# Low halves of split weight tiles: an engine subtraction, or a copy and an accumulating DMA

## The chip, the cores and the metric

The kernel runs on one core of one Trainium2 chip. A core has a matrix engine (TensorE, PE in the profile), two elementwise engines (VectorE or DVE, ScalarE or ACT), a programmable engine (GpSimd or POOL) and SyncE (SP), which here only issues DMAs. Each takes its instructions in the order of the program; an instruction that has to wait holds up everything behind it on its engine. DMAs can be issued from SP, ACT or GpSimd; all of them are carried out by the core's 16 DMA engines.

The metric is the device time of one execution in microseconds (us), the median of repeated runs.

## The reference

A trunk of two decoder layers over 512 tokens of width 1024, in float32. What the chip spends its time on is cut to this:

```
layer 0:  u = rmsnorm(x);  proj = u @ w_in            # 1024 -> 7200 columns
          y = SSD scan (16 heads);  o = forgetting attention (16 heads)
          x = x + rmsnorm(concat(y, o) @ w_out)       # 2048 -> 1024
layer 1:  u = rmsnorm(x);  val, gate, z = split(u @ w_in)   # 1024 -> 3 * 2048
          h = val * sigmoid(gate)
          h = causal depthwise conv, 31 taps, over 2048 channels
          h = silu(layernorm(h)) * silu(z)
          x = x + rmsnorm(h @ w_out)                  # 2048 -> 1024
```

## The kernel before, in words

**Split products.** TensorE multiplies here in the rounded type float32r. To keep float32 accuracy each operand is split in two: `hi`, its rounding, and `lo = value - hi`. A product is three matmuls: hi by hi, hi by lo, lo by hi (`mm3`). Activations are split as they are made, weights as they are loaded, so every weight tile (128 partitions x 1024 elements, 512 KB) goes this way: SP issues its load into a raw buffer `wr` (`wload`, L124); ACT rounds it into the first half of a tile `w` (L107, a CAST); DVE or GpSimd subtracts, `w[lo] = wr - w[hi]` (L108); PE reads both halves. The table of jobs says which engine subtracts: DVE and GpSimd by turns in layer 0, mostly DVE in layer 1 (`ENG1 = V`, `GLO`). Twelve half-size tiles `ws` at the border of the layers are treated alike.

**Buffers.** Raw tiles come from a pool of two buffers. `w` tiles share a pool of seven with other tiles of 8 KB per partition (the gate inputs `zs` and `sz`, attention weights `ph` and `pl`, at the start the input `x` and scratch `junk`). A raw buffer is free when both the rounding and the subtraction have read it. `split_to` calls for the splits of the next two jobs, or more, ahead of the job that runs, at a raised priority (`HP`).

**Jobs and order.** The products are a list of jobs, one weight tile each, mostly 24 matmuls. PE's order is written by hand; the other engines' orders are made by a scheduler from priorities, at build time. Beside the jobs run "chains", stepped a fixed number of steps per chunk of products: the scan and the attention in layer 0, and in layer 1 the convolution. The convolution's taps are dealt out: DVE adds taps in PSUM (L723, L727), ACT multiplies and GpSimd adds others in SBUF (L666 and L681), a few go to PE. When all 16 channel tiles are done, their sums (L749, L753) give the layer norm's statistics (L813 to L826), and only then can the last product, by `w_out`, begin.

**Stages**, by the profile's time: start 0 to 60 us; layer 0's projections with scan and attention 60 to 555; its output product 555 to 616; border of the layers to 674; layer 1's projections with the convolution 674 to 1003 (called *the convolution stage* below); the statistics to 1016; the last product to 1101; the end.

At the start x's rows are normalized, transposed by PE (`uT`) and split by ACT and DVE into eight pairs `uh`, `ul` (L236, L237), numbered uh_123 to uh_130 in the listings below. PE's first product (`dtf`) needs all eight in turn.

Of the kernel before, what the change touches and what calls it, by code (L numbers as in the profile page):

```python
# [12 lines left out]
ALU = mybir.AluOpType  # L13
# [3 lines left out]
S = 512  # L17
# [19 lines left out]
def trunk(  # L37
# [7 lines left out]
    V, G, A, T = nc.vector, nc.gpsimd, nc.scalar, nc.tensor  # L45
# [3 lines left out]
    cp = ctx.enter_context(tc.tile_pool(name="const", bufs=1))  # L49
    rp = ctx.enter_context(tc.tile_pool(name="raw", bufs=2))  # L50
    qp = ctx.enter_context(tc.tile_pool(name="q", bufs=7))
# [54 lines left out]
    def split(hi, lo, src, hi_eng, lo_eng):  # L106
        hi_eng(hi, src)  # L107
        lo_eng.tensor_tensor(lo, src, f32(hi), ALU.subtract)  # L108
# [11 lines left out]

    # ---------------------------------------------------------------- weight tiles, loaded and split ahead of their use
    def wload(w, r0, nk, c0, n):
# [3 lines left out]
        return raw  # L126

    def wsplit(raw, nk, n, eng, small=False):
        if small:
            hl = [[t2("ws", F32R) for _ in range(2)] for _ in range(2)]  # L130
            for i in range(2):
                split(hl[0][i], hl[1][i], raw[:, i * S : (i + 1) * S], A.copy, eng)
            return [lambda k, t=t: t[k // 4][:, k % 4 * P : (k % 4 + 1) * P] for t in hl]
        hl = q8("w", [2, 1024])
        split(hl[:, 0, : nk * n], hl[:, 1, : nk * n], raw[:, : nk * n], A.copy, eng)
        v = hl[:, :, : nk * n].rearrange("p a (k f) -> p a k f", k=nk)
        return [lambda k, a=a: v[:, a, k, :] for a in range(2)]

    jobs = []
# [28 lines left out]
    def chunks():  # L168
        """Runs the next job, one chunk of products a step."""
        i = state["run"]  # L170
        split_to(i + 1)
        first = True
        for _ in jobs[i].run(*jobs[i].w):
            if first:
                split_to(i + 1 + ahead.get(i, 2))
                first = False
            yield
        state["run"] = i + 1
# [3 lines left out]
    def run(n, chain=None, pace=0.0):  # L182
        """Runs n jobs; after each chunk `pace` steps of the chain on average."""
        for _ in range(n):
            for _ in chunks():
                debt[0] += pace
                while debt[0] >= 1.0:
                    debt[0] -= 1.0
                    if chain is not None and next(chain, None) == "wait":
                        debt[0] = 1.0 - pace  # L190
                        break
# [4 lines left out]

    # ---------------------------------------------------------------- norms
    def rstd_of(ss, n):
# [13 lines left out]
    def scaled(dst, xs):  # L212
        """dst = xs / rms(xs), xs being the parts of the rows."""
        s2 = col("s2", 2)
        for i, t in enumerate(xs):
            sumsq(t, s2[:, i : i + 1])
        if len(xs) == 2:
            V.tensor_tensor(s2[:, 0:1], s2[:, 0:1], s2[:, 1:2], ALU.add)
        r = rstd_of(s2[:, 0:1], D)
        for t, u in zip(xs, dst):  # L220
            V.tensor_scalar(u, t, r, None, ALU.mult)
# [16 lines left out]

    # ---------------------------------------------------------------- inputs and constants
    xq = [q8("x", [2, D], F32) for _ in range(2)]  # L240
# [28 lines left out]

    # dt and forget-gate columns of the input projection  # L270
    raw = rp.tile([P, 1024], F32, tag="wr", name=nm("wr"))
# [45 lines left out]
    def conv_columns():  # L317
        v3 = t2("v3")
        nc.sync.dma_start(v3[:124, :].rearrange("p (a c) -> p a c", a=4),
                          o_conv_w[0].rearrange("k (t c) -> (k t) c", c=P).rearrange("(a p) c -> p a c", p=124))  # L320
        yield
        pb = bank("cw")
        for a in range(4):
            T.transpose(pb[:, a * 124 : (a + 1) * 124], v3[:124, a * P : (a + 1) * P], ident[:124, :124])
        V.tensor_copy(cw, pb[:, :496])
        # a shift common to all channels leaves the layer norm as it is: take the bias' mean out
        bm = col("bm")
        V.tensor_reduce(bm, c1[:, o_cb1 : o_cb1 + 16], AX.X, ALU.add)
        pb = bank("bm")
        mm(pb[:, 0:1], ones, bm, True, True)  # L330
        bs = col("bs")
        V.tensor_scalar(bs, pb[:, 0:1], -1.0 / 2048, None, ALU.mult)
        V.tensor_scalar(c1[:, o_cb1 : o_cb1 + 16], c1[:, o_cb1 : o_cb1 + 16], bs, None, ALU.add)
        yield

    # ---------------------------------------------------------------- jobs of layer 0
    uh = [t2("uh", F32R) for _ in range(KT)]
# [107 lines left out]

    # ---- layer norm / residual end of a layer
    RES = 6
# [4 lines left out]
    def out_proj(w, stages, nk, gpost, resid, done, hooks):  # L452
        """stages: (fn, lead) pairs; the last fn(k) gives (hi, lo) of the k-th 128 rows of the contraction."""
        hl = {}
# [79 lines left out]

    # ---- the order of layer 0
    for kind in ("B", "C", "x"):
# [40 lines left out]

    # ---------------------------------------------------------------- layer 0, start
    # ---------------------------------------------------------------- jobs of layer 1
    NT = 16  # L580
# [54 lines left out]
    def tap_job(j):  # L635
        """The first taps of a tile as products with diagonal matrices."""
        n = NPE[j // 2]
# [19 lines left out]
    def pool_adds(js, s0, n, init):  # L657
        """Taps s0..s0+n-1 of the tiles js, in turn, into partial sums."""
        a2 = {}
# [146 lines left out]
    def stats1():  # L806
        # layer norm statistics: per token, then over all partitions
        pb = bank("st")
# [43 lines left out]

    # ---------------------------------------------------------------- layer 0
    split_order = []
# [29 lines left out]

    # softplus / log-sigmoid, decays
    def row(s, dt=F32):
# [30 lines left out]
    V.tensor_tensor_scan(cs, keep, da, 0.0, ALU.mult, ALU.add)  # L917
    # rows 0-15: decay sums, 32-47: forget sums, 64-79: their negatives; (hi, lo) pairs
    chl = cp.tile([80, 2, S], F32R, name="chl")
# [3 lines left out]
    V.tensor_scalar(chl[64:80], f32(chl)[32:48], -1.0, None, ALU.mult)  # L923
    # rows stacked for one transpose per chunk: dt, -cs, exp(end - cs), exp(cs)
    stk = t2("stk")
# [15 lines left out]
    def decay_chain():  # L941
# [3 lines left out]
        V.tensor_copy(tk, pb.rearrange("p (c f) -> p c f", c=NB))  # L945
        # chunk decay, the same on every partition
        pb = bank("cd")
# [15 lines left out]
    def prep(g):  # L963
        """Token-major inputs of a group of four heads."""
        def hb(q, c0):
# [257 lines left out]

    # ---------------------------------------------------------------- layer 1
    if MAN1:
# [59 lines left out]
```

## Time and profile before

| | |
|---|---|
| median of 3 runs | 1092.64 us (1091.94 to 1094.2) |
| span of the profiled execution, from the first to the last instruction | 1111.2 us |
| PE, DVE, ACT, POOL busy in it | 978.9, 750.4, 552.9, 545.1 us |
| granted TensorE clock, mean | 0.933 |
| weight rounding on ACT (L107, full tiles) | 130 x 1.05 us |
| weight subtraction (L108, full tiles) | DVE 81, 155.0 us; GpSimd 49, 121.2 us |
| DMA engines' share of busy time | 24.2% |

The span is the profiled execution's time: the profile has no other. It is 18.6 us over the median of the unprofiled runs. Times within the span are from its start. In a table of instructions "idle before" is how long the engine stood still ahead of them, with what ended the wait; idle time of an engine that nobody waits for costs nothing.

### The profile page before, as it was taken

How to read it: one execution, taken by the hardware profiler on the slowest of the kernel's cores; microseconds unless marked ns; L12 is line 12 of the kernel's file. 1: busy time of each engine (PE TensorE's matmuls, PEld its weight loads, DVE VectorE, ACT ScalarE, POOL GpSimd, SP SyncE). 2: the span in 40 equal slices, each digit the busy share in tenths (PEclk: the TensorE clock that was granted, in tenths of full speed). 3: DMA queues.
4: the chain of work that ended last, by engine and by line, in shares of the span. 5: the costliest groups of instructions: out<-in, count | busy, mean ns of one | idle time of the engine just before them, and what ended most of it. 6: DMA issues, size and time to landing. Idle time of an engine off the chain costs nothing.

```text
span 1111.2 us, 13506 instructions
## 1 busy us (share of the span) xinstructions
PE 978.9 (88%) x4823; PEld 793.9 (71%) x4823; DVE 750.4 (68%) x1144; ACT 552.9 (50%) x999; POOL 545.1 (49%) x443
## 2 busy tenths in 40 slices
PE   4998989989979989998999999999386985876997
PEld 3886768767867868786788888888264853664886
DVE  3646674766546756565632559988999989978813
ACT  4445635464625445454543347657273793535520
POOL 3225252535323334334433108988767997736720
PEclk7998989999989999998999999999697988976999
DMA  6313120222210212121244314141112310221312
GB/s 178 111 44 111 40 57 24 72 75 62 73 48 20 62 55 76 40 78 39 83 142 132 100 53 119 58 114 43 49 42 76 100 33 0 76 95 38 133 58 76
DMA packets 113352, 80.13 MB, mean 72 GB/s; under 512 B 5052, under 2 KB 99908, under 8 KB 113284
## 3 DMA queue, kind: packets, MB, share of 16 engines
q1 hardware_dynamic: 112788, 79.17, 24.2%
q8 instruction: 38, 0.62, 0.2%
q14 instruction: 30, 0.25, 0.1%
q10 hardware_dynamic: 496, 0.09, 0.0%
HBM read 77.02 MB, written 2.10 MB: 71 GB/s over the span
## 4 chain that ended last, share of the span: by engine, by line
PE 28%; DVE 19%; issue 7%; POOL 4%; ACT 4%; DMA 1%; DVEq 0%; POOLq 0%; ACTq 0%
PE o L96 16%; DVE acc L727 9%; PE m L96 8%; DVE w L108 5%; PE tm L96 2%; DVE acc L723 2%; POOL acc L681 2%; PE s L96 1%; DMA wr<-in_o_w_in_dram 1%; PE pT L1179 1%; ACT junk L209 1%; ACT prod L666 1%; ACT w L107 1%; POOL Qsum L753 1%; POOL w L108 1%
## 5 line engine op out<-in xcount | busy, mean ns | idle before, releaser
L96 PE MATMUL m<-uh,w 128*128 128x512 f32 (+1 forms) x1360 | 457.0, 403 | 56.8 <-DVE w L108 28.8
L96 PEld LDWEIGHTS m<-uh,w 128*128 128x128 f32 x1360 | 262.7, 196 | 115.5 <-DVE w L108 30.8
L96 PE MATMUL m<-ul,w 128*128 128x512 f32 (+1 forms) x680 | 267.6, 394 | 0.0
L681 POOL TENSOR_TENSOR acc<-acc,prod 128x510 f32<-128x510 f32 (+19 forms) x160 | 212.9, 1367 | 28.2 <-ACT prod L666 28.2
L108 POOL TENSOR_TENSOR w<-wr,w 128x1024 fp32r<-128x1024 f32 x49 | 121.2, 2473 | 208.2 <-ACT w L107 207.7
L107 ACT CAST w<-wr 128x1024 fp32r<-128x1024 f32 x130 | 135.3, 1048 | 158.1 <-DMA wr<-in_o_w_in_dram 74.5
L108 DVE TENSOR_TENSOR w<-wr,w 128x1024 fp32r<-128x1024 f32 x81 | 155.0, 1917 | 62.0 <-ACT w L107 61.9
L727 DVE SCALAR_TENSOR_TENSOR acc<-h,cw,acc 128x496 f32<-128x496 f32 (+19 forms) x282 | 185.3, 725 | 0.7
L96 PE MATMUL o<-w,hlh 128*128 128x512 f32 x512 | 164.0, 402 | 11.5 <-ACT hlh L107 11.5
L96 PEld LDWEIGHTS m<-ul,w 128*128 128x128 f32 x680 | 133.5, 196 | 21.5 <-issue 0.5
L96 PEld LDWEIGHTS o<-w,hlh 128*128 128x128 f32 x512 | 96.7, 194 | 31.1 <-ACT hlh L107 12.3
L96 PE MATMUL o<-w,hll 128*128 128x512 f32 x256 | 102.1, 399 | 1.1 <-POOL hll L108 0.6
L666 ACT ACTIVATE prod<-h,cw 128x510 f32<-128x510 f32 (+19 forms) x160 | 102.0, 708 | 0.0
L1169 POOL TENSOR_SCALAR pr<-pr,ri 128x128 f32<-128x128 f32 (+1 forms) x64 | 35.1, 549 | 131.8 <-DVE ri L1168 121.5
L96 PE MATMUL tm<-w,uh 128*128 128x256 f32 (+1 forms) x384 | 94.8, 338 | 3.0 <-DVE cv L359 3.0
L96 PEld LDWEIGHTS tm<-w,uh 128*128 128x128 f32 x384 | 64.8, 197 | 9.3 <-issue 4.8
L91 ACT ACTIVATE pr<-s,nmx 128x128 f32<-128x128 f32 (+1 forms) x64 | 33.8, 528 | 71.4 <-DVE nmx L1163 65.0
L96 PE MATMUL tm<-w,ul 128*128 128x256 f32 (+1 forms) x192 | 62.5, 326 | 0.0
L202 POOL TENSOR_TENSOR rstd<-var,mhalf 128x1 f32<-128x1 f32 (+1 forms) x20 | 13.3, 667 | 93.0 <-DVE var L200 92.8
L96 PEld LDWEIGHTS o<-w,hll 128*128 128x128 f32 x256 | 49.2, 192 | 12.9 <-DVE hll L108 1.3
L359 DVE SCALAR_TENSOR_TENSOR cv<-m,c,cv 128x511 f32<-128x511 f32 (+2 forms) x48 | 35.0, 742 | 10.2 <-ACT cv L357 9.8
L96 PEld LDWEIGHTS tm<-w,ul 128*128 128x128 f32 x192 | 37.4, 195 | 2.8
(262 smaller groups left out, 1515.6 us busy)
## 6 DMA issues: line engine op xcount, KB each, us to landing
wr<-in_e_w_in_dram SPq DMA_DIRECT2D x56, 512.0 KB
wr<-in_o_w_in_dram SPq DMA_DIRECT2D x48, 512.0 KB
wr<-in_e_w_out_dram SPq DMA_DIRECT2D x16, 512.0 KB
wr<-in_o_w_out_dram SPq DMA_DIRECT2D x16, 512.0 KB
x<-in_x_dram SPq DMA_DIRECT2D x4, 512.0 KB
x<-in_x_dram SPq DMA_DIRECT2D x8, 256.0 KB
out_dram<-o SPq DMA_DIRECT2D x4, 256.0 KB
out_dram<-y SPq DMA_DIRECT2D x4, 256.0 KB
```

What stands on the lines that cost most here:

```text
L91: i = A.activation(*a, **kw)
L96: T.matmul(o, l, r, start=start, stop=stop, skip_group_check=True)
L107: hi_eng(hi, src)
L108: lo_eng.tensor_tensor(lo, src, f32(hi), ALU.subtract)
L202: G.tensor_tensor(r, v, mhalf.to_broadcast([P, ss.shape[-1]]), ALU.pow)
L209: A.activation(junk[:, :n], src, AF.Square, accum_out=ss)
L359: V.scalar_tensor_tensor(acc[:, s:], pb[:, : S - s], w[3 - s], acc[:, s:], ALU.mult, ALU.add)
L666: A.activation(prs[i][:, s:], hs[j][:, : S - s], AF.Copy, scale=w31(30 - s, j))
L681: G.tensor_tensor(a2[j][:, s:], a2[j][:, s:], prs.pop(i)[:, s:], ALU.add)
L723: V.scalar_tensor_tensor(a[:, s:], h[:, : S - s], w31(30 - s, j), a2[:, s:], ALU.mult, ALU.add)
L727: V.scalar_tensor_tensor(a[:, s:], h[:, : S - s], w31(30 - s, j), a[:, s:], ALU.mult, ALU.add)
L1169: G.tensor_scalar(p[:, :L], p[:, :L], ri, 1.0, ALU.mult, ALU.mult)
```

## The change

After it, `lo` is made in two steps. ACT writes the rounding with its sign turned into the low half, then a DMA issued from GpSimd adds the raw tile to it: `lo = -round(raw) + raw`. So ACT passes twice over every weight tile, DVE and GpSimd no longer subtract weights, and GpSimd issues a DMA that moves within SBUF, reading the raw tile and the low half and writing the low half. The argument `eng`, which named the subtracting engine, has no effect any more. The raw pool has three buffers in place of two. A raw buffer is now free when the DMA has landed. Splits of activations (`split`, `hilo`) stay as they were. The rest of the change is comments that went.

```diff
-    rp = ctx.enter_context(tc.tile_pool(name="raw", bufs=2))
+    rp = ctx.enter_context(tc.tile_pool(name="raw", bufs=3))
...
+    def wpair(hi, lo, raw):
+
+        A.copy(hi, raw)
+        A.mul(lo, raw, -1.0)
+        G.dma_start(lo, raw, accum_op=ALU.add)
+
     def wsplit(raw, nk, n, eng, small=False):
         if small:
             hl = [[t2("ws", F32R) for _ in range(2)] for _ in range(2)]
             for i in range(2):
-                split(hl[0][i], hl[1][i], raw[:, i * S : (i + 1) * S], A.copy, eng)
+                wpair(hl[0][i], hl[1][i], raw[:, i * S : (i + 1) * S])
             return [lambda k, t=t: t[k // 4][:, k % 4 * P : (k % 4 + 1) * P] for t in hl]
         hl = q8("w", [2, 1024])
-        split(hl[:, 0, : nk * n], hl[:, 1, : nk * n], raw[:, : nk * n], A.copy, eng)
+        wpair(hl[:, 0, : nk * n], hl[:, 1, : nk * n], raw[:, : nk * n])
```

The scheduler makes new orders from it; PE's is the same. Two places follow. The listings give each instruction as line, operation, tile written <- tiles read, size; in the changed kernel all lines from the helper on stand six lower.

**ACT at the start, before.** Weight roundings (w_218, w_223, w_228) stand singly among the splits of x:

```order
L107 CAST w_218<-wr_145 128x1024
L236 ACTIVATE uh_125<-uT_191,c_111 128x256
L107 CAST w_223<-wr_221 128x1024
L236 ACTIVATE uh_126<-uT_191,c_111 128x256
L236 ACTIVATE uh_127<-uT_200,c_111 128x256
L236 ACTIVATE uh_128<-uT_200,c_111 128x256
L236 ACTIVATE uh_129<-uT_209,c_111 128x256
L107 CAST w_228<-wr_226 128x1024
L236 ACTIVATE uh_130<-uT_209,c_111 128x256
```

**ACT at the start, now**, a little further on, from uh_126; w_218, w_224 and w_230 have had both passes ahead of uh_125:

```order
L242 ACTIVATE uh_126<-uT_191,c_111 128x256
L215 ACTIVATE junk_269,s_50_268<-x_76 128x1024
L242 ACTIVATE uh_127<-uT_200,c_111 128x256
L130 CAST w_485<-wr_234 128x1024
L131 ACTIVATE w_485<-wr_234 128x1024
L130 CAST w_556<-wr_489 128x1024
L131 ACTIVATE w_556<-wr_489 128x1024
L130 CAST w_562<-wr_560 128x1024
L131 ACTIVATE w_562<-wr_560 128x1024
L242 ACTIVATE uh_128<-uT_200,c_111 128x256
L242 ACTIVATE uh_129<-uT_209,c_111 128x256
L242 ACTIVATE uh_130<-uT_209,c_111 128x256
```

Both passes over six weight tiles, where there were three single ones, now stand ahead of uh_128, uh_129 and uh_130. The raw buffers are taken in the order wr_107 (a smaller weight), wr_145, wr_222, then wr_228 in the first, wr_234 in the second, wr_489 in the third and wr_560 in the first again.

**GpSimd in the convolution stage, before.** Tap additions, the first sums of two finished tiles, and one weight subtraction:

```order
L681 TENSOR_TENSOR acc_1285_6493<-acc_1285_6493,prod_6503 128x510
L681 TENSOR_TENSOR acc_1286_6496<-acc_1286_6496,prod_6505 128x510
L681 TENSOR_TENSOR acc_1285_6493<-acc_1285_6493,prod_6520 128x509
L681 TENSOR_TENSOR acc_1286_6496<-acc_1286_6496,prod_6530 128x509
L681 TENSOR_TENSOR acc_1285_6493<-acc_1285_6493,prod_6542 128x508
L681 TENSOR_TENSOR acc_1286_6496<-acc_1286_6496,prod_6556 128x508
L749 TENSOR_TENSOR Ssum_6574<-cvo_6340,cvo_6434 128x512
L749 TENSOR_TENSOR Qsum_6575<-sq_6553,sq_6572 128x512
L681 TENSOR_TENSOR acc_1285_6493<-acc_1285_6493,prod_6583 128x507
L681 TENSOR_TENSOR acc_1286_6496<-acc_1286_6496,prod_6594 128x507
L108 TENSOR_TENSOR w_6773<-wr_6722,w_6773 128x1024
```

**GpSimd there, now:**

```order
L132 DMA w_6756<-wr_6716 128x1024
L687 TENSOR_TENSOR acc_1286_6587<-acc_1286_6587,prod_6596 128x510
L687 TENSOR_TENSOR acc_1285_6584<-acc_1285_6584,prod_6612 128x509
L687 TENSOR_TENSOR acc_1286_6587<-acc_1286_6587,prod_6622 128x509
L687 TENSOR_TENSOR acc_1285_6584<-acc_1285_6584,prod_6634 128x508
L132 DMA w_6814<-wr_6760 128x1024
L687 TENSOR_TENSOR acc_1286_6587<-acc_1286_6587,prod_6648 128x508
L755 TENSOR_TENSOR Ssum_6667<-cvo_6428,cvo_6524 128x512
L755 TENSOR_TENSOR Qsum_6668<-sq_6645,sq_6665 128x512
L687 TENSOR_TENSOR acc_1285_6584<-acc_1285_6584,prod_6676 128x507
L132 DMA w_6869<-wr_6818 128x1024
```

A DMA issue stands after about every four additions; from the first addition of the stage to its statistics there are 38 of them, and six more just ahead. Each of them stands in GpSimd's queue until ACT has made its second pass.

## The prediction

> **What bounds the kernel now.** I read the busy time by stretch first. Columns: stretch, its length, busy us and count on PE, PE's weight loads, DVE, ACT and POOL, granted clock, DMA share, GB/s.
>
> ```profile
> 0.00:60.00 60.00, 44.57 (x265) 38.14 (x266) 28.22 (x47) 27.26 (x43) 19.09 (x30) 0.89 0.50 137
> 60.00:310.00 250.00, 228.33 (x1131) 181.78 (x1130) 157.41 (x270) 135.30 (x229) 96.53 (x58) 0.96 0.22 61
> 310.00:555.00 245.00, 230.58 (x1347) 189.65 (x1348) 148.66 (x303) 114.79 (x271) 92.26 (x117) 0.97 0.19 56
> 674.00:1003.00 329.00, 268.23 (x1085) 210.12 (x1083) 302.59 (x356) 188.67 (x306) 265.33 (x192) 0.88 0.23 65
> 1016.00:1101.00 85.00, 85.00 (x368) 70.28 (x369) 44.67 (x53) 30.82 (x49) 36.46 (x20) 0.98 0.22 78
> ```
>
> In layer 0 (60 to 555) and in the last product PE works nearly all the time, so freed DVE time is worth little there. In the convolution stage (674 to 1003) DVE is busy for 302.6 of 329 us, GpSimd for 265.3, and PE stands still for 61. Next the groups of instructions within that stage:
>
> ```profile
> L727 DVE SCALAR_TENSOR_TENSOR acc<-h,cw,acc 128x484 f32<-128x484 f32 (+20 forms) x270 | 176.6, 724 | 0.4
> L108 DVE TENSOR_TENSOR w<-wr,w 128x1024 fp32r<-128x1024 f32 x34 | 89.7, 2643 | 6.5 <-ACT w L107 6.5
> L723 DVE SCALAR_TENSOR_TENSOR acc<-h,cw,acc 128x501 f32<-128x501 f32 (+1 forms) x10 | 26.8, 2709 | 0.1
> ...
> L681 POOL TENSOR_TENSOR acc<-acc,prod 128x510 f32<-128x510 f32 (+19 forms) x160 | 212.9, 1367 | 28.2 <-ACT prod L666 28.2
> L753 POOL TENSOR_TENSOR Qsum<-Qsum,sq 128x512 f32<-128x512 f32 x12 | 17.8, 1482 | 0.9 <-ACT sq L744 0.7
> L753 POOL TENSOR_TENSOR Ssum<-Ssum,cvo 128x512 f32<-128x512 f32 x12 | 17.7, 1475 | 24.4 <-ACT cvo L742 17.3 <-DVE cvo L732 6.9
> L108 POOL TENSOR_TENSOR w<-wr,w 128x1024 fp32r<-128x1024 f32 x5 | 14.4, 2885 | 7.3 <-ACT w L107 7.3
> ```
>
> The 34 weight subtractions take DVE 89.7 us, a mean of 2.64, though over the whole kernel the median (the middle one of the three numbers here) is 1.23. The timeline shows why:
>
> ```profile
> L108 DVE TENSOR_TENSOR w<-wr,w x81: 1209/1226/22058, 16.0 to 1064.6; 128x1024 fp32r<-128x1024 f32 x81
> ...
> 775.86 22.06 DVE L108 TENSOR_TENSOR w<-wr,w 128x1024 fp32r<-128x1024 f32 x1
> 776.10 20.73 POOL L681 TENSOR_TENSOR acc<-acc,prod 128x507 f32<-128x507 f32 x17
> ```
>
> One subtraction of two SBUF tiles lasted as long as GpSimd's run of 17 additions without a pause. L727, whose accumulator lies in PSUM, is never held so. The waits of the stage and of layer 0:
>
> ```profile
> PE m L96 <- DVE w L108: 28.8, 4, 11.8
> ...
> POOL rstd L822 <- DVE va L820: 5.2, 1, 5.2
> ```
> ```profile
> PE st L96 <- POOL hll L108: 3.7, 4, 1.4
> ...
> PE cb L96 <- POOL hll L108: 3.0, 4, 1.1
> ...
> PE yd L96 <- POOL hll L108: 2.0, 2, 1.1
> ```
>
> PE waits 28.8 us for subtracted weights, and all of it is in this stage; in layer 0 no wait for a weight tile is listed, only for scan and attention tiles. So the stage is set by DVE, and by a DVE that GpSimd holds up.
>
> **The change part by part.** Removed: all weight subtractions. In the stage DVE falls from 302.6 to about 213, below PE's 268, and no longer sets the end. GpSimd loses 14.4 us.
>
> *GpSimd in the stage.* These rows price what it keeps and what it gains:
>
> ```profile
> L681 POOL TENSOR_TENSOR acc<-acc,prod x160: 1223/1274/2292, 674.4 to 972.6; 128x511 f32<-128x511 f32 x14, 128x510 f32<-128x510 f32 x14, 128x509 f32<-128x509 f32 x14, 128x508 f32<-128x508 f32 x14
> ...
> L108 POOL TENSOR_TENSOR w<-wr,w x49: 2354/2400/3424, 19.3 to 1069.1; 128x1024 fp32r<-128x1024 f32 x49
> ...
> L124 SPq DMA_DIRECT2D wr<-in_o_w_in_dram x48: 367/368/536, 585.0 to 953.5; - x48
> ...
> L202 POOL TENSOR_TENSOR rstd<-var,mhalf 128x1 f32<-128x1 f32 (+1 forms) x20 | 13.3, 667 | 93.0 <-DVE var L200 92.8
> ```
>
> Kept: 160 additions at their undisturbed median of 1.274, 203.8; the sums 17.8 + 17.7 + 2 x 1.3 for the first pair, 38.1; the statistics' 1.2; together 243. Added: 38 DMA issues between the first addition and the statistics. No DMA is issued by GpSimd before, so the cost x of an issue is unknown. Below: 0.37, what SP needs to issue a tile of this size. Above: 2.40, a whole pass of GpSimd over the tile. GpSimd is a programmed engine that must describe 128 rows, yet touches none of their elements; I take the middle, 1.4, an estimate: 38 x 1.4 = 53. Waiting: before, 66 us of the stage (28.2 + 0.9 + 24.4 + 7.3 + 5.2). The 24 us for the sums came from a late DVE and go, as do the 7.3; I keep the 5.2, half of the 28.2 behind ACT (14), and 6 for issues that arrive before ACT's second pass, 25. Then 243 + 53 + 25 = 321 instead of 329: **-8 us**. GpSimd, not DVE, is now the bound, and since weights leave through its queue, PE follows its pace. The ends: 243 + 14 + 25 = 282 (-47) and 243 + 91 + 25 = 359 (+30).
>
> The Trainium skill, DMA: Bandwidth & Descriptors, section "Latency and other measured facts", gives about 1 us until the first byte of a DMA issued from GpSimd, and puts it down to descriptor emission by its cores. If that is all an issue occupies, the stage comes to 243 + 38 + 25 = 306, -23, and the whole to about -9; no run here shows it yet, and that page prices a plain DMA, not one that adds.
>
> *The start.* The second pass and the DMA both stand in a chain here:
>
> ```profile
> 14.96 1.05 ACT L107 CAST w<-wr 128x1024 fp32r<-128x1024 f32 x1 [0.38 <-DMA wr<-in_e_w_in_dram]
> 15.91 0.47 ACT L236 ACTIVATE uh<-uT,c 128x256 fp32r<-128x256 f32 x1
> 18.13 1.04 ACT L107 CAST w<-wr 128x1024 fp32r<-128x1024 f32 x1 [1.75 <-DMA wr<-in_e_w_in_dram]
> ...
> 22.16 0.48 ACT L236 ACTIVATE uh<-uT,c 128x256 fp32r<-128x256 f32 x1
> ```
> ```profile
> 24.43 0.41 PE L96 MATMUL m<-uh,w 128*128 128x256 f32 x1
> ```
> ```profile
> 721.12 3.85 DMA wr<-in_o_w_in_dram
> ...
> 943.70 5.29 DMA wr<-in_o_w_in_dram
> ```
>
> Before, ACT starts the last split of x (uh_130) at 22.16 and PE its first weight product at 24.43. Now three tiles of two passes each run from 14.96 to 21.3 (their loads are there by 18.1). uh_128 stands behind six passes whose raw tiles load into the buffers of those three, and each of these is free only when its accumulating DMA has landed. Let A be the time from GpSimd's turn to landing. First DMA at 17.1; its buffer free at 17.1 + A; load 3.85 (the shorter row); passes until 23.1 + A. The second until 25.2 + A, the third 27.3 + A. Two splits of 0.47 later uh_130 starts at 28.2 + A: **6.0 + A** late. A from below: 3.85, a plain load of as many bytes. From above: 10.6, two reads as long as the longer load, 5.29. I take 5.3: **+11 us** (+9.9 to +16.6). PE has nothing else to run, and behind it PE is the bound, so nothing gives this back.
>
> *Layer 0 and the border.* The same 54 full tiles are rounded here:
>
> ```profile
> L107 ACT CAST w<-wr 128x1024 fp32r<-128x1024 f32 x54 | 56.2, 1049 | 26.4 <-PE o L96 11.3 <-PE m L96 9.2 <-DMA wr<-in_e_w_out_dram 3.1
> ```
>
> ACT gets 56 us more on 250 of 495. The cover is that tiles are called for two jobs ahead: 24 products at 85 / 368 = 0.231 us are 5.5, two jobs 11 us, against 2.1 + 5.3 for passes and DMA. If that cover were gone, each tile would cost PE what it is late. But PE's 36 us of standing still (21.7 + 14.4) are ends of chains through ACT, DVE and GpSimd: queued behind a DMA that waits for ACT are GpSimd's `hll` and `pr`, for which the scan's and the attention's products wait. If ACT's 23% more work lengthens all of these waits by that share it is +8; if the subtractions' going ends GpSimd's share of them, 3.7 + 3.0 + 2.0 in the rows above, -9. I take **+3**. In the last product 48 of the 85 us are free on GpSimd and 54 on ACT: nothing.
>
> *Sum.* +11 - 8 + 3 = **+6** on the span of 1111.2 us, 0.54%. That execution is 18.6 us longer than the median of the three runs; the same share of 1092.64 gives **1098.5 us**.
>
> **The rivals.** *Issuing is cheap.* If GpSimd issues a DMA in the time of its smallest operations, 0.667 in the row of L202, the stage is 243 + 25 + 25 = 293, -36; with +11 and +3 the whole is -22, about 1071. For it: the issue moves no data through GpSimd. Against: for each of 128 rows two reads and a write have to be described. It decides below x = 1.2, where the sum turns negative.
>
> *The landing is slow.* If two reads and a write follow each other, A is 3 x 5.29 = 15.9. Late in the stage the pool of seven leaves three buffers to `w` (four hold `sz`), so a tile's turn is product 5.5, two passes 2.1, about 2 in GpSimd's queue and 15.9, over three: 8.5 us per tile. For the stage's 39 tiles (34 + 5 subtractions) that is 332, with PE's own tap products 354, +25; the start costs +22, the rest +3: +50, about 1142.
>
> ```profile
> L96 PE MATMUL acc<-h,dg 128*128 128x512 f32 (+10 forms) x44 | 22.1, 665 | 2.8 <-DVE h L608 2.8
> ```
>
> It decides from A = 11, where landing no longer fits under two jobs. For it: no row shows an adding DMA. Against: the 16 engines are busy 23% of the stage, so their time is there.
>
> *It cancels.* At x about 1.2, stage and start offset each other and the time stays within 0.2%, about what a measurement of this kernel can tell from no change.
>
> **How the numbers follow.** The forecast, GpSimd the new bound and a late start, 0.48; of it 0.37 slower, 0.07 within 0.2%, 0.04 faster. Cheap issuing 0.36: 0.35 faster, 0.01 the same. Slow landing 0.16, all slower. Together faster 0.39, same 0.08, slower 0.53. The likeliest case's own range, x from 1.2 to 1.9, is 1092 to 1117. The ends of all costs are -47 + 10 - 9 = -46 and +30 + 17 + 8 = +55, with the slow landing inside them; cutting the outer tenth on both sides, **1058 to 1142**.
>
> **What would show it.** Right: ACT's last split of x near 33 and PE's first weight product near 35; in the convolution stage POOL with the fewest idle us and DVE no longer held for longer than one L723; POOL's additions at about 1.27; waits of PE there named after the DMA into `w` or after POOL. x is the gap between the additions around an issue, A the time from the issue to the first reader or the next load. Wrong: POOL still idle for 60 us in the stage, a gap under 1 us or over 2.4, a first weight product before 30, or PE waiting for weights in layer 0.

## The result and the profile after

The changed kernel takes **1188.43 us** (median of four, 1171.08 to 1193.36) where the kernel before takes 1093.42 in runs beside it: 1.0756 times as long, 95% interval 1.0658 to 1.0854. The forecast was 1098.5, its range ended at 1142: the sign was right, the size was not. Ratios here and below are of undisturbed executions alone, while medians and the profile (of a disturbed execution of 1191.35 us) are of any: the ratio gives +83 us, the medians +95. The profile's span is 1189.3, 78 more than the span that the prediction was reckoned against and 93 more than that of a second profile of the kernel before (e9).

By stretch, with the columns of the prediction's first listing (length, busy us of PE, weight loads, DVE, ACT, POOL, clock, DMA share, GB/s); in the order of the program: start, scan part of layer 0, attention part with the first tiles of the output product, the rest of that product and the border, convolution stage; then, after the statistics, the last product.

```profile
0.00:73.00 73.00, 44.30 (x268) 37.75 (x269) 27.07 (x53) 41.55 (x62) 16.18 (x35) 0.84 0.78 182
73.00:330.00 257.00, 221.09 (x1050) 174.94 (x1049) 116.56 (x235) 147.25 (x229) 79.19 (x69) 0.92 0.51 113
330.00:593.00 263.00, 243.89 (x1420) 202.05 (x1419) 128.78 (x295) 145.52 (x311) 84.98 (x131) 0.94 0.44 102
593.00:740.00 147.00, 118.08 (x610) 100.71 (x609) 36.26 (x75) 63.10 (x113) 25.96 (x34) 0.91 0.70 157
740.00:1074.00 334.00, 266.57 (x1088) 209.31 (x1086) 251.21 (x326) 231.13 (x355) 269.06 (x229) 0.89 0.59 131
...
1087.00:1176.00 89.00, 83.00 (x356) 67.67 (x356) 35.61 (x44) 42.00 (x61) 26.78 (x26) 0.95 0.61 141
```

Over the whole span PE is busy for 986.3 us (978.9 before): nearly all of the loss is time in which it stands still. DVE's busy time fell from 750.4 to 612.6 and GpSimd's from 545.1 to 510.8; ACT's rose from 552.9 to 679.1, and the DMA share, 0.19 to 0.50 in the prediction's stretches, is 0.44 to 0.78 in these. What was to be measured of the new instructions: the rows of the line that issues the DMA (durations in ns, shortest, median and longest), then from the page the groups, the issues with their median landing, and the queues.

```profile
L132 POOL DMA_DIRECT2D w<-wr x130: 837/868/2264, 16.2 to 1151.7; - x130
...
DMA to landing us min/median/max: 3.3/5.3/8.8
```
```profile
L131 ACT ACTIVATE w<-wr 128x1024 fp32r<-128x1024 f32 x130 | 137.2, 1056 | 0.0
...
L132 POOL DMA_DIRECT2D w<-wr x130 | 129.0, 996 | 368.9 <-ACT w L131 326.7 <-PE pT L1185 13.2 <-ACT HH L107 10.8
...
L729 DVE SCALAR_TENSOR_TENSOR acc<-h,cw,acc 128x501 f32<-128x501 f32 (+1 forms) x10 | 58.4, 5856 | 0.1
...
w<-wr POOLq DMA_DIRECT2D x130, 512.0 KB, 5.5
...
q0 software_dynamic: 20448, 71.31, 33.3%
q1 hardware_dynamic: 112788, 79.17, 22.4%
```

An issue is cheap. The landing is near the 5.3 that was taken: the first fence's median of 5.3 is of full and half-size tiles together, that of the full tiles alone is 5.5. And yet 33.3% of the DMA engines' time goes to the adding DMAs, more than to all loads (22.4%). L729 is the L723 of before, a tap of two SBUF tiles: 58.4 us, 26.8 before. PE's longest waits (waiting engine, line and tile, what it waited for: us in total, times, longest):

```profile
PE uT L235 <- DVE u L227: 25.8, 3, 19.8
...
PE m L96 <- DVE h L614: 22.7, 1, 22.7
...
PE m L96 <- DMA w<-wr: 16.7, 4, 11.0
PE m L96 <- ACT sg L91: 15.8, 3, 12.0
...
PE xt L994 <- ACT cv L91: 13.7, 4, 9.9
```

Two of these in the kernel before:

```profile
PE uT L229 <- DVE u L221: 3.1, 2, 1.7
...
PE xt L988 <- ACT cv L91: 2.8, 2, 1.9
```

Of the five waits after, only one names the DMA. The others are waits for chain work on DVE and ACT.

PE's matmuls come in the same order in all kernels here, 4823 recorded each time, so the start of the n-th marks the same point of work. This gives the length of each part in each profile, worked out from the rows' times (marks: matmuls 200, 1300, 2800, 3400 and 4400; the first column begins with the first matmul and the last one ends with the last, so the ends of the span are not in it). The rows e1 to e16 are the experiments. Each row is one profile.

```
                                 start   scan  attention  border  convolution  last product
                                               + product             stage
before, profile of the forecast   45.8  247.1    273.8    116.8     309.0        109.2
before, again (e9)                44.6  250.0    273.9    117.4     289.0        110.5
changed kernel                    58.3  266.7    284.5    141.1     314.4        114.8
e1  third raw buffer              49.3  248.4    277.9    117.9     284.9        110.7
e2  two passes, no DMA            53.2  278.0    281.0    117.1     292.6        118.7
e3  change in layer 0             60.8  268.6    284.6    122.6     285.4        110.8
e4  change in layer 1             50.2  247.6    277.0    126.2     312.6        116.3
e5  negation on DVE               52.5  238.9    275.9    138.1     333.6        109.0
e6  border on the engines         60.5  266.8    278.1    122.9     310.7        114.4
e7  x loaded early                60.0  272.0    284.4    134.1     313.7        114.5
e8  no taps of two SBUF tiles     58.8  271.6    284.3    136.7     293.6        114.5
e10 four raw buffers              57.2  265.2    278.0    133.5     290.0        113.3
e11 e8's taps, kernel before      43.5  248.4    271.5    116.8     306.0        110.8
e12 half the stage's tiles        45.7  250.0    273.9    117.5     330.8        109.2
e13 layer 0, negation on DVE      51.8  240.9    283.2    116.8     286.5        110.4
e14 layer 0, all on DVE           51.4  245.0    274.6    116.8     284.3        109.8
e15 e7 and e10                    57.9  263.4    284.6    122.2     291.3        113.1
e16 e14 with two raw buffers      45.3  241.7    271.2    117.0     288.0        109.2
```

Against the second profile of before, the change costs 13.7 at the start, 16.7 in the scan part, 10.6 in the attention part, 23.7 at the border, 25.4 in the stage and 4.3 at the end: 94, of one profile that is longer than the ratio tells. Three readings carry the rest.

**Scan part.** ACT in the changed kernel (start, us, ..., in brackets the idle time before), and the same place before:

```profile
98.33 0.63 ACT L91 ACTIVATE cv<-cv 128x512 f32<-128x512 f32 x1
104.78 1.04 ACT L130 CAST w<-wr 128x1024 fp32r<-128x1024 f32 x1 [5.81 <-DMA wr<-in_e_w_in_dram]
105.73 1.05 ACT L131 ACTIVATE w<-wr 128x1024 fp32r<-128x1024 f32 x1
106.69 1.03 ACT L130 CAST w<-wr 128x1024 fp32r<-128x1024 f32 x1
107.62 1.05 ACT L131 ACTIVATE w<-wr 128x1024 fp32r<-128x1024 f32 x1
108.58 1.65 ACT L91 ACTIVATE cv<-cv 128x512 f32<-128x512 f32 x3
```
```profile
82.53 1.15 ACT L91 ACTIVATE cv<-cv 128x512 f32<-128x512 f32 x2
83.59 1.04 ACT L107 CAST w<-wr 128x1024 fp32r<-128x1024 f32 x1
84.53 0.62 ACT L91 ACTIVATE cv<-cv 128x512 f32<-128x512 f32 x1
85.81 1.05 ACT L107 CAST w<-wr 128x1024 fp32r<-128x1024 f32 x1 [0.65 <-DMA wr<-in_e_w_in_dram]
86.77 0.62 ACT L91 ACTIVATE cv<-cv 128x512 f32<-128x512 f32 x1
```

Before, the four activations that the scan's transposes need went in between single roundings. Now two tiles of two passes stand ahead of three of them, the first pass waits 5.81 for its load, and PE's `xt` waits 13.7 us for `cv`, 2.8 before.

**Border.** SP, ACT, DVE and PE in the changed kernel:

```profile
633.40 44.16 SPq L124 DMA_DIRECT2D wr<-in_o_w_in_dram  x9
677.66 19.29 SPq L118 DMA_DIRECT2D x<-in_x_dram  x8
```
```profile
640.12 0.62 ACT L130 CAST ws<-wr 128x512 fp32r<-128x512 f32 x1 [6.70 <-DMA wr<-in_o_w_in_dram]
...
655.81 0.62 ACT L130 CAST ws<-wr 128x512 fp32r<-128x512 f32 x1 [9.51 <-DMA wr<-in_o_w_in_dram]
...
670.81 0.62 ACT L130 CAST ws<-wr 128x512 fp32r<-128x512 f32 x1 [8.63 <-DMA wr<-in_o_w_in_dram]
...
672.90 0.57 ACT L215 ACTIVATE junk<-o 128x512 f32<-128x512 f32 x1
...
682.06 0.75 DVE L533 SCALAR_TENSOR_TENSOR o<-o,rstd,x 128x512 f32<-128x512 f32 x1 [7.53 <-DMA x<-in_x_dram]
```

Nine weight loads take SP 44 us, since each waits for a raw buffer; the residual x stands behind them and is issued only at 677.66. ACT's sums of squares (`junk`) stand behind half-size passes that wait 6.70, 9.51 and 8.63 us. With both late, `u` is late, and PE's `uT` waits 25.8 us for it, 19.8 of them at once (3.1 before).

**Convolution stage.** GpSimd, then DVE:

```profile
802.48 0.85 POOL L132 DMA_DIRECT2D w<-wr  x1
803.10 7.77 POOL L687 TENSOR_TENSOR acc<-acc,prod 128x510 f32<-128x510 f32 x6
810.57 1.14 POOL L132 DMA_DIRECT2D w<-wr  x1
```
```profile
835.59 16.78 DVE L729 SCALAR_TENSOR_TENSOR acc<-h,cw,acc 128x501 f32<-128x501 f32 x1
...
877.22 22.85 DVE L729 SCALAR_TENSOR_TENSOR acc<-h,cw,acc 128x501 f32<-128x501 f32 x1
...
901.91 0.68 DVE L614 TENSOR_TENSOR h<-m,sg 128x512 f32<-128x512 f32 x1
```
```profile
902.64 0.79 PE L96 MATMUL m<-uh,w 128*128 128x512 f32 x1 [22.71 <-DVE h L614]
```

From the start of an issue to the next addition is 0.62 us; the rows' own lengths overlap. GpSimd runs without a gap here, and does so again from 835.70 and from 877.54, when DVE taps that take 0.74 undisturbed last 16.78 and 22.85 us. Behind the second of them in DVE's queue stands a gated product `h`, and PE has stood still for 22.71 us when it gets it.

### The profile page after: what moved, and what is told of

Read it like the earlier page. It is cut to its first block, busy times and chain, and to the rows that moved or that the text cites. A ratio compares the mean times of both kernels' runs of the same rounds, so it can differ in the third digit from the quotient of the medians.

```text
span 1189.3 us, 13917 instructions
## 1 busy us (share of the span) xinstructions
PE 986.3 (83%) x4823; PEld 799.6 (67%) x4823; DVE 612.6 (52%) x1057; ACT 679.1 (57%) x1141; POOL 510.8 (43%) x530
## 3 DMA queue, kind: packets, MB, share of 16 engines
q0 software_dynamic: 20448, 71.31, 33.3%
q1 hardware_dynamic: 112788, 79.17, 22.4%
## 5 line engine op out<-in xcount | busy, mean ns | idle before, releaser
L132 POOL DMA_DIRECT2D w<-wr x130 | 129.0, 996 | 368.9 <-ACT w L131 326.7
L687 POOL TENSOR_TENSOR acc<-acc,prod 128x510 f32<-128x510 f32 (+19 forms) x160 | 220.2, 1859 | 13.2 <-ACT prod L672 13.2
L733 DVE SCALAR_TENSOR_TENSOR acc<-h,cw,acc 128x493 f32<-128x493 f32 (+19 forms) x282 | 184.5, 724 | 11.2 <-ACT acc L725 10.2
L131 ACT ACTIVATE w<-wr 128x1024 fp32r<-128x1024 f32 x130 | 137.2, 1056 | 0.0
L729 DVE SCALAR_TENSOR_TENSOR acc<-h,cw,acc 128x501 f32<-128x501 f32 (+1 forms) x10 | 58.4, 5856 | 0.1
```

The source lines that it names most:

```text
L131: A.mul(lo, raw, -1.0)
L132: G.dma_start(lo, raw, accum_op=ALU.add)
L687: G.tensor_tensor(a2[j][:, s:], a2[j][:, s:], prs.pop(i)[:, s:], ALU.add)
L729: V.scalar_tensor_tensor(a[:, s:], h[:, : S - s], w31(30 - s, j), a2[:, s:], ALU.mult, ALU.add)
L733: V.scalar_tensor_tensor(a[:, s:], h[:, : S - s], w31(30 - s, j), a[:, s:], ALU.mult, ALU.add)
```

## The experiments

**Where the loss lies: e3 and e4.** The change in one layer alone, with three raw buffers:

```diff
+        if state["split"] < J1:      # e4: >= J1
+            A.copy(hi, raw)
+            A.mul(lo, raw, -1.0)
+            G.dma_start(lo, raw, accum_op=ALU.add)
+        else:
+            split(hi, lo, raw, A.copy, eng)
...
```

`state["split"]` is the number of the job whose tile is split, and `J1` the first job of layer 1; `JO` and `JO1` below are the first jobs of the two output products, and `NSMALL` is the six jobs with half-size tiles. In this and the later diffs the lines that hand `eng` on to `wpair`, and some that go, are left out.

> Two passes and the adding DMA for the weight tiles of layer 0 alone (its start included, and its output product); layer 1's tiles, the twelve half-size ones at the border included, are rounded once and subtracted as before, with three raw buffers. Theory T: start +13, layer 0 about +30, a part of the border's 26: 1135 to 1160 us. The prediction's own sum, with its +11 and +3 for these places: 1105 to 1110 us.

> The same for the tiles of layer 1 alone, the half-size ones at the border included; layer 0 as before, with three raw buffers. Theory T: the border keeps most of its 26, the convolution stage loses up to 10: 1110 to 1130 us. The prediction's own sum, -8 for the stage and nothing at the border: about 1085 us.

Measured: e3 1142.52 (1.0433, 1.0364 to 1.0502), e4 1135.93 (1.0295, 1.0184 to 1.0405). By the ratios that is +47 and +32; with the third buffer (+4, e1) counted once it is 75 of the 83. Both are far above the prediction's own sums, and inside the ranges of theory T (the turn of a raw buffer, which the adding DMA makes long; e1's expectation below has it in full) if e4 is taken by its ratio, about 1128. The places are not T's, though: in e4 28 us lie in the convolution stage (312.6 against e1's 284.9; e6 and e7 have 310.7 and 313.7), where T had up to 10, and the border's 24 comes in neither half alone, 5 in e3 and 8 in e4 over e1.

**The buffers and ACT's second pass: e1, e2, e5.**

```diff
-    rp = ctx.enter_context(tc.tile_pool(name="raw", bufs=2))     # e1, this alone
+    rp = ctx.enter_context(tc.tile_pool(name="raw", bufs=3))
```
```diff
         A.mul(lo, raw, -1.0)                                      # e2, in wpair
-        G.dma_start(lo, raw, accum_op=ALU.add)
+        eng.tensor_tensor(lo, raw, f32(lo), ALU.add)
```
```diff
-        A.mul(lo, raw, -1.0)                                      # e5
+        V.tensor_scalar(lo, raw, -1.0, None, ALU.mult)
```

> The kernel before with a third raw buffer and nothing else; subtractions stay on the engines. Theory T (the loss is the turn of a raw buffer, which the adding DMA makes long, and the work that stands in order behind ACT's passes and SP's loads): the third buffer by itself costs nothing, 1085 to 1098 us. Rival O (the order that the scheduler makes with other buffers is the loss): 1120 us or more.

> The changed kernel, three buffers and both passes of ACT, but DVE or GpSimd adds the raw tile to the low half in place of the DMA. Rival R1 (ACT's second pass, 130 more passes of about 1.05 us, is the loss): 1150 to 1185 us. Theory T: the raw buffer is free again about 2 us after the second pass, so most of the loss is gone, 1095 to 1120 us, of which the start has about +4.

> The changed kernel with the negated copy made by DVE (the raw tile times -1) instead of ACT's second pass; the adding DMA and three raw buffers stay. Theory P (in layer 0 the loss is ACT's second pass, which stands in ACT's queue ahead of the scan's activations; at the border it is the DMA): layer 0 gives back some 25 of its +31, the rest stays, 1150 to 1168 us. Theory T (the turn of the raw buffer through the DMA, everywhere): little changes, 1178 to 1192 us.

Measured: e1 1099.01 (1.0041, 1.001 to 1.0072), e2 1147.4 (1.0484, 1.0408 to 1.0561), e5 1160.73 (1.0605, 1.0542 to 1.0668). Without a single adding DMA, e2 loses 52 us, a little under the range of rival R1 and far over theory T's: T, that the turn of the raw buffer is the loss, falls as the main cause. It falls for layer 0 from the other side as well: e5 keeps every DMA and its scan part takes 238.9, less than before (250.0), while e2's takes 278.0. PE's wait for the scan's activations in e2, and in e5:

```profile
PE xt L994 <- ACT cv L91: 9.7, 3, 7.2
```
```profile
PE xt L994 <- ACT cv L91: 0.9, 1, 0.9
```

So in the scan part it is ACT's second pass, with the DMA (266.7) or without (278.0). In the attention part the third buffer (4.0, e1) and the second pass (3.1 more, e2) make 7 of the 10.6. Against the changed kernel e5 gives back 28 in the scan part, 9 in the attention part and 6 at the start. It gives nothing back at the border (138.1) and loses 19 in the stage. e1 shows that the third buffer alone costs 4.7 at the start: six full tiles are rounded there ahead of the last split of x, where three were.

**The border: e6, e7, e10, e15.**

```diff
-                wpair(hl[0][i], hl[1][i], raw[:, i * S : (i + 1) * S])            # e6, half-size tiles
+                split(hl[0][i], hl[1][i], raw[:, i * S : (i + 1) * S], A.copy, eng)
```
```diff
+            if k2 == 0: xs.extend(resid(b) for b in range(NB))                    # e7, in second()
...
-            xr = resid(b)
+            xr = xs[b]
```
```diff
-    rp = ctx.enter_context(tc.tile_pool(name="raw", bufs=3))                      # e10; e15 has both
+    rp = ctx.enter_context(tc.tile_pool(name="raw", bufs=4))
...
-    tp = ctx.enter_context(tc.tile_pool(name="t", bufs=62))
+    tp = ctx.enter_context(tc.tile_pool(name="t", bufs=60))
```

> The changed kernel, but the twelve half-size tiles at the border of the layers are rounded once and subtracted by DVE and GpSimd as before. If the border's +25 comes from the wait for raw buffers that the adding DMA holds: 15 to 22 less than the changed kernel, 1163 to 1175 us. If it comes from traffic of the large tiles' DMAs around it: 1183 to 1192 us.

> The changed kernel, but the loads of the residual x (eight of 256 KB) stand in SP's queue ahead of the border's weight loads instead of behind all of them; nothing else. If the border waits for x alone: 15 to 22 less, 1165 to 1175 us. If ACT's sums of squares, which stand behind its passes, are as late by themselves: 3 to 10 less, 1178 to 1186 us. If the border's loss is neither: 1186 to 1192 us.

> The changed kernel with a fourth raw buffer (and two tiles fewer in the pool of 62, which by itself leaves every engine's order as it was). If the border's loss is the turn of the raw buffers through the DMA: the border gives back 8 to 18 us, the start and layer 0 little, 1165 to 1180 us. If the loads are slow because the adding DMAs take the DMA engines: 1184 to 1192 us.

> e7 and e10 at once: the changed kernel with x loaded ahead of the border's weights and four raw buffers. If these two waits make up the border's loss: border 141 - 7 - 8 = 126 us or less, the whole 1143 to 1152 us. If a third thing does (ACT's sums behind its passes, however early their tiles come): the border stays above 130 us and the whole at 1150 to 1156 us.

Measured: e6 1168.19 (1.0653, 1.0571 to 1.0736), its border 122.9: 18 of the 24 hang on the way the half-size tiles take, and as e2, with both passes but no DMA, loses nothing there (117.1), on their DMAs. e7 1188.28 (1.0828, 1.0749 to 1.0907): its border is 7 shorter, but the scan part, whose code the edit does not touch, came out 5 longer, as it did in e8, so one profile can be off by that much in a part; the whole did not move. e10 1152.0 (1.0534, 1.0507 to 1.0561): 8 less at the border, 6 in the attention part, and 24 in the stage, which was not expected. e15 1143.78 (1.0422, 1.0362 to 1.0481), border 122.2: the two waits together are 19 of the 24, more than the 7 and 8 apiece, as it must be where `u` needs both. In e15 the eight loads of x take SP 7 us and stand ahead of most of the weights, and `uT` waits little:

```profile
626.95 6.69 SPq L118 DMA_DIRECT2D x<-in_x_dram  x8
...
PE uT L235 <- DVE u L227: 6.2, 3, 5.4
```

**The convolution stage: e8, e9, e11, e12.**

```diff
-                V.tensor_copy(a[:, :s], a2[:, :s])                                 # e8; e11, e12 have it too
-                V.scalar_tensor_tensor(a[:, s:], h[:, : S - s], w31(30 - s, j), a2[:, s:], ALU.mult, ALU.add)
+                V.tensor_copy(a, a2)
+                V.scalar_tensor_tensor(a[:, s:], h[:, : S - s], w31(30 - s, j), a[:, s:], ALU.mult, ALU.add)
```
```diff
+        if J1 + NSMALL <= state["split"] < JO1 and state["split"] % 2 == 1:        # e12
+            A.copy(hi, raw)
+            A.mul(lo, raw, -1.0)
+            G.dma_start(lo, raw, accum_op=ALU.add)
+        else:
+            split(hi, lo, raw, A.copy, eng)
```

> The changed kernel, but the ten DVE taps that read two SBUF tiles (58.4 us in its profile, 24.5 in the kernel before with three raw buffers) are made another way: DVE first copies GpSimd's partial sum whole into PSUM, and the tap then adds in PSUM like the others. Ten copies of a whole tile more. If the convolution stage is long because GpSimd, which no longer pauses, holds these taps: the stage gives back 20 to 30 us, 1158 to 1170 us. If the stage is set by ACT's second pass or by late weights: 1183 to 1192 us.

> The kernel before once more, for a second profile. The one shown before was 18.6 us longer than the median of its runs. If that lies in the convolution stage, where DVE was held: a span near 1092 to 1100 us, DVE's subtractions of two SBUF tiles and its taps L723 held for less than 116 us in all, the stage 15 to 20 us shorter, all other stages the same to 2 us. If it lies elsewhere, the stage is as long as it was.

> The kernel before (two raw buffers, subtractions on the engines), with only the ten taps of two SBUF tiles made as in e8. DVE gives up about 20 us of being held and takes ten copies of about 0.6 us: if DVE still sets the stage, 1078 to 1086 us. If the held time only moves on to the weight subtractions, which are two-SBUF-tile operations too: 1089 to 1096 us.

> e11, with the adding DMA for every second full weight tile of the convolution stage alone (20 tiles, all taken from DVE; ACT passes over these twice); two raw buffers; start, layer 0, border and last product as before. If DVE's work and holds set the stage and 20 issues at 0.62 us are cheap: the stage near PE's own 268 to 280, 1060 to 1076 us. If late weights or ACT's passes take their place: 1080 to 1095 us.

Measured: e8 1167.55 (1.0669, 1.0612 to 1.0726), the stage 293.6 where it was 314.4. The ten taps, which now add in PSUM, are never held:

```profile
L729 DVE SCALAR_TENSOR_TENSOR acc<-h,cw,acc x10: 729/736/744, 830.7 to 984.2; 128x501 f32<-128x501 f32 x8, 128x497 f32<-128x497 f32 x2
```

So by the profiles some 20 of the stage's 25 were these holds: the stage is 310.7 to 314.4 in four profiles with the ten taps held for 51 us (the changed kernel, e4, e6, e7), and 290.0 to 293.6 in the three with 31 or none (e10, e15, e8). The gain in the whole is less sure, 21 us by the medians and 10 by the ratios, whose intervals overlap. With the holds gone PE's largest wait in the stage is for the DMA into `w`, 34.7 us where it was 16.7. e9 (the kernel before; 1095.94 in its own runs, span 1096.0) has a stage of 289.0 and all else within 3 us of the first profile: what made that one long lies in the stage, 20 us, and DVE's full-tile subtractions took 131.4 us instead of 155.0.

e11 gave 1102.93 (1.0024, 0.9985 to 1.0063): no change, where 1078 to 1086 was expected if DVE set the stage. In its profile (span 1106.6) no tap is held, but the 81 subtractions take 163.5 us, 131.4 in e9. e12 gave 1135.48 (1.0381, 1.0357 to 1.0405) against 1060 to 1076, the largest miss of the study. Its rows show why:

```profile
L108 DVE TENSOR_TENSOR w<-wr,w 128x1024 fp32r<-128x1024 f32 x61 | 161.7, 2650 | 72.8 <-ACT w L107 72.6
...
L731 DVE SCALAR_TENSOR_TENSOR acc<-h,cw,acc 128x501 f32<-128x501 f32 (+1 forms) x10 | 7.1, 736 | 0.0
```

With 20 subtractions fewer and no tap held, the 61 that were left took about as much as all 81 in e11, and more than in e9: **while others of its kind are left, holds are not removed with the instruction that is held; the next one meets GpSimd's runs.** Held time, worked out over the whole kernel as the busy time of DVE's full-tile operations (subtractions; in e5 the negations) and of these taps over their undisturbed medians (1.226, 0.694 and 0.736), beside the stage:

```
                e2     e9     e16    e1     e11    before  e12    e5       e8     e10    e6     e7     changed
held, us        46     51     52     57     64     75      87     98        0     31     51     51     51
stage, us      292.6  289.0  288.0  284.9  306.0  309.0   330.8  333.6    293.6  290.0  310.7  313.7  314.4
```

Left, kernels with DVE passes over the stage's weights; right, kernels with the DMA and ACT's second pass for all of them. On the left 46 to 57 us of holds make no difference to the stage, 64 and 75 go with 21 and 24 more than e1's, 87 and 98 with 46 and 49; on the right the first 31 make none, and the next 20 go with 17 to 24. That holds cause it rests on e8, whose edit is aimed at them alone; e12 changed ACT's and GpSimd's order too. How e10's fourth buffer came to meet fewer holds (taps 38.8 instead of 58.4) was not tested.

**Is the DMA good in layer 0, and is there a better kernel: e13, e14, e16.** After the first six tiles, up to the output product, without ACT's second pass:

```diff
+        if 6 <= state["split"] < JO:
+            V.tensor_scalar(lo, raw, -1.0, None, ALU.mult)                         # e13, three raw buffers
+            G.dma_start(lo, raw, accum_op=ALU.add)
+        else:
+            eng.tensor_tensor(lo, raw, f32(hi), ALU.subtract)
```
```diff
+            V.tensor_tensor(lo, raw, f32(hi), ALU.subtract)                        # e14 three, e16 two raw buffers
```

> Three raw buffers; in layer 0's projections alone (after the first six tiles, up to its output product) DVE makes the negated copy and the adding DMA finishes it; everywhere else one rounding and engine subtractions. If the DMA with a single ACT pass is good for the scan's part, as in e5: that part 237 to 242 us where the kernel before has 250, the whole 1084 to 1093 us. If e5's gain there hung on something else: 248 or more, 1097 to 1106 us.

> As e13, but DVE subtracts in one operation and there is no DMA: in layer 0's projections GpSimd is rid of its subtractions, with three raw buffers. If e5's gain came from freeing GpSimd: the scan's part 237 to 243 us as well, 1084 to 1093 us. If it needs the DMA: near 248, as in e1, 1095 to 1102 us.

> e14 with two raw buffers, so the kernel before with DVE in GpSimd's place for layer 0's subtractions. If freeing GpSimd shortens the scan's part: 1080 to 1090 us, faster than both kernels. If DVE's own chain work then waits behind the subtractions: 1094 to 1105 us.

Measured: e13 1103.06 (1.0049, 1.0012 to 1.0086): the scan part 240.9 as hoped, but the attention part 283.2, 9 more than before, for a reason not followed up, and so the whole missed its 1084 to 1093. e14 1091.73 (0.9962, 0.9924 to 0.9999), scan part 245.0. **e16 1085.45 (0.9906, 0.9873 to 0.994)** is 0.9% faster than the kernel before: scan part 241.7, attention part 271.2, the start as before. A gain like e5's in layer 0 is therefore had without the DMA: scan and attention parts together take 512.9 in e16, 514.8 in e5 and 523.9 in e9. With three buffers in both, the scan part is 4 shorter with the DMA (e13) than without (e14), so some of e5's gain there may be the DMA's. Whether e16 gains by what GpSimd no longer has to do, or because DVE subtracts a tile in 1.29 us where GpSimd took 2.40, was not told apart. Its DVE row for layer 0 is undisturbed at a mean of 1.286:

```profile
L131 DVE TENSOR_TENSOR w<-wr,w 128x1024 fp32r<-128x1024 f32 x50 | 63.8, 1286 | 44.2 <-ACT w L129 44.1
```

## Why the prediction was wrong

**The start: right in mechanism and nearly in size.** Forecast +11; measured 12.5 against the profile of the forecast. ACT's last split of x came at 36.10 where "near 33" was given, PE's first weight product at 37.61 instead of 35, for one reason: the loads.

```profile
22.34 0.46 ACT L242 ACTIVATE uh<-uT,c 128x256 fp32r<-128x256 f32 x1
29.01 1.04 ACT L130 CAST w<-wr 128x1024 fp32r<-128x1024 f32 x1 [6.21 <-DMA wr<-in_e_w_in_dram]
...
36.10 0.47 ACT L242 ACTIVATE uh<-uT,c 128x256 fp32r<-128x256 f32 x1 [0.58 <-DVE ul L243]
```

By the trace GpSimd issued the first DMA at 16.18 and it landed at 20.87, so A was 4.7 here. SP issued the load into its buffer at 20.92, and ACT could begin at 29.01: 8.1 us where the sum had 3.85, in a stretch in which the DMA engines are busy 0.78 of the time. The makeup differs too: of the 13.7 against e9, 4.7 are the third buffer's, 3.9 the second pass's (e2) and 5.1 the DMA's.

**Layer 0 and border, +3: the step that failed.** Measured, by the parts of the table: +20 in the scan part and +11 in the attention part (17 and 11 against e9), +24 at the border. The prediction took the distance of two jobs as cover: a weight tile is called for 11 us ahead, so a dearer preparation doesn't show. That looked at who waits for the tile, and indeed PE hardly waits for a tile there: the 16.7 us for the DMA lie in the stage. It did not ask **who stands behind the passes on ACT**: what is queued behind a waiting instruction was named for GpSimd (`hll`, `pr`), and not for ACT, where the scan's activations and the border's sums are, nor for SP, where x is loaded. The 23% more work on ACT was priced as if spread evenly over the waits; it comes in blocks of two and three tiles, placed ahead of chain work. The +3 itself was taken from between -9 and +8 without a working. e2 and e5 show the second pass as the cause in the scan part; e6 and e15 show the wait for raw buffers, with x and ACT's sums behind it, as the border's. Each of these edits also lets the scheduler make new orders, so whether another order of the same passes would have cost less stays open.

**Convolution stage, -8: wrong in mechanism and in its base.** Measured +5 against the first profile and +25 against e9. That GpSimd is now the bound does not hold: the terms of its sum were 243 + 53 + 25; measured are 269 busy, issues included, and 65 idle. Idle time over 60 us and a gap under 1 us were two of the prediction's own signs of being wrong. x is 0.62, not 1.4, which is inside the bounds and close to the 0.667 of the rival of cheap issuing; by that rival the stage should have gained 36. "DVE no longer held for longer than one L723": this is the false statement. L723 was read as the one kind that is left and would stay at its mean of 2.7. With the 34 subtractions gone the ten taps, now L729, were held for 51 us instead of 19. GpSimd's longest unbroken run is no longer than before, but it has more long ones: worked out from the starts of its instructions (a run ends where the next one starts later than the last one's usual length allows), seven of over 15 us in the changed kernel and two in e9, the longest 31.7 and 37.8. Run lengths alone don't decide, since e10 has four of over 26 us and taps held for 31; the issues on GpSimd at 840.66 and 848.66 fall inside the hold of 16.78 and end nothing. And a lone profile was taken for the kernel: its stage was 20 us longer than e9's, with 75 us of holds instead of 51.

The Trainium skill, SBUF — State Buffer, section "SBUF: two separate sides", says that GpSimd's operations and DVE's with two SBUF inputs, or in a mode of two ports, share a port pair by an exclusive lock, held for a whole instruction. The runs agree on which are held: taps from two SBUF tiles up to 22.9 us, from PSUM at most 0.744 (e8), and in e5 the one-input negation too (median 0.694, longest 10.7). They differ on how long: 16.78 us is some twelve additions, not one, and 22.06 us in the kernel before were seventeen. The negations of e5 (shortest, median and longest in ns), and the taps of the changed kernel:

```profile
L131 DVE TENSOR_SCALAR w<-wr x130: 622/694/10739, 14.5 to 1118.5; 128x1024 fp32r<-128x1024 f32 x130
```
```profile
L729 DVE SCALAR_TENSOR_TENSOR acc<-h,cw,acc x10: 822/1778/22852, 827.4 to 1003.4; 128x501 f32<-128x501 f32 x8, 128x497 f32<-128x497 f32 x2
```

The Trainium skill, DMA: Bandwidth & Descriptors, section "Latency and other measured facts", gave about 1 us to the first byte, and by it the prediction had a stage of 306. The issue occupied 0.62, and the stage was 334: the price was near enough, and decided nothing.

**The last product, nothing: +4** against e9, and none in e5 (109.0), while e2 has +8 (118.7): so ACT's second pass here as well. **The rival of slow landing** gave 1142, nearest to the result, and for the wrong reason: it decides from A = 11, and A was 5.5.

## What to carry to other kernels

A preparation pass that moves to an engine with half its time free is free only if nothing with an earlier deadline stands behind it in that engine's queue; list what is queued behind each new or moved instruction on every engine that issues one, the load queue included, before trusting a distance of jobs ahead. Where one engine's runs hold another's instructions, do not count the held time of one kind of instruction as gained when that kind is removed: while others of the kind are left, the hold can pass to them, and may grow. Take a second profile of the kernel before, if its first is off the median by more than the effect that is looked for.

## What the runs showed that was not expected

A DMA that adds within SBUF costs GpSimd only 0.62 us for 512 KB, and it lands in 5.5 us (median; 4.5 to 8.8 by the trace), but 71 MB of such traffic take 33.3% of the DMA engines' time, where 79 MB of loads and the rest take 22.4%. Loads beside it slow down: where ACT's rounding waited for its load, the median from SP's issue to the rounding, worked out from the traces, is 4.0 us in e9 (38 loads), 4.2 in e2, which has no adding DMA (10), and 7.3 in the changed kernel (28). An issue on GpSimd did not break a hold of DVE. And a third raw buffer by itself, which looked harmless, costs 0.4% (e1), 4.7 us of it at the start, where it lets three more tiles of weight work ahead of the first products.
